# Retention's values by seven products of halves, and GpSimd as issuer of three kinds of transfers

## The chip, the cores and the metric

One core of a Trainium2 chip runs the whole program in one launch. The metric is the device time of one execution in microseconds, as the median of several runs.

## The reference

Two blocks over 512 tokens of width 1024, all in float32. The first is one hybrid layer (gated MLP mixing, sparse attention, a linear recurrence, then a feed-forward network of width 2816). The second is two hybrid layers, and the change lies in those. Each of them does, cut to what matters:

```python
proj = h @ w_in
qa, ka, va, za, qr, kr, vr, zr, ga, gr = jnp.split(proj, SPLIT_POINTS, axis=-1)
# attention: three groups (window, dilation) of four heads, values va (512 x 1536)
y_att = o_att.reshape(B, S, ATT_OUT) * jax.nn.silu(za)
# retention: four heads, values vr (512 x 1024), 256 per head
o_ret = retention(qr, kr, vr, positions, ret_gn_w)
y_ret = o_ret * jax.nn.silu(zr)
merged = jax.nn.sigmoid(ga) * (y_att @ w_proj_attn) + jax.nn.sigmoid(gr) * (y_ret @ w_proj_ret)
return x + gate[:, None, :] * (merged @ w_out)
```

The change concerns `vr = h @ w_vr`: 512 tokens by 1024 inputs by 1024 outputs, once per layer.

## The kernel before, in words

**Precision.** Every large product is made of three matmuls: each operand is held as a rounded high half and a low half (`split`, L140: ScalarE writes the high half, L144; VectorE subtracts it from the source for the low one, L145), and high x high, high x low and low x high are added in PSUM. `load_w` (L188) brings one weight tile of 128 x 1024 (512 KB) by SP into a raw buffer `wr` and splits it into `wh` and `wl`, of which there are four. It runs at a higher priority, so weights are loaded and split some way ahead. Where a stage lends a pool (`self.rawp`), two of three raw tiles come from there, four more buffers.

**Two shapes of a product.** `F_` (L204) makes one tile of 128 outputs by 512 tokens: 8 slices of k x 3 matmuls, 24 for one weight tile. `T_` (L231) makes 512 tokens by 512 outputs in four PSUM banks: 8 slices x 4 token tiles x 3 = 96 matmuls on four weight tiles.

**Seven products of halves.** `TS_` (L311) makes 512 tokens by 1024 outputs from operands cut in halves of the tokens, of the inputs and of the outputs, by Winograd's form of Strassen's scheme: seven products of 256 tokens x 512 inputs x 512 outputs, each 2 weight tiles x 2 token tiles x 2 slices x 3 = 24 matmuls. Three of them work on the operand and the weights as they are, four on sums. The order is written out by hand at its end:

```python
product("a", A(0, 0), B(0, 0), True, lambda t, ps: nc.scalar.activation(e[t], ps, AF.Copy))
product("d", A(1, 1), Tx(3), True)
product("a", A(1, 0), B(0, 1), False, lambda t, ps: done(t, 0, ps))
product("b", Sx(1), Tx(1), True, lambda t, ps: add(u[t], e[t], ps))
product("c", Sx(0), Tx(0), True, p5)
product("b", Sx(2), Tx(2), False, p7)
product("a", Sx(3), B(1, 1), True, p3)
```

VectorE adds the products together (L343 to L359), six additions per token tile. Before, only the strided values of attention (`strided_v`, L1066, the second and third group of `va`) are made so. The sums of the operand (`H`, four sums in two halves each) are made there by GpSimd and VectorE (L1078 to L1086) and split. The sums of the weights are made beforehand: `weight_sums` (L364) loads four quarter tiles `q` by SP, does four subtractions on GpSimd (L375 to L378) and writes the results to DRAM by SP (L381), in four groups per pair of weights, with pauses between the steps that the caller gives (12, 16 and 12 in the feed-forward stage).

**Order of the work.** Side work is written as generators (`spawn`, `tick`); each yields the pause until its next step, on a clock that counts matmuls, and is stepped between matmuls of the main line. The instructions of each engine, and the transfers of each queue, are issued in one order that is fixed when the program is built. A later tile that takes the room of an earlier one waits for its last reader.

**Stages that matter here.** The first block's feed-forward (`ffn`, L826) runs 44 `F_` passes; beside it run `ada` (L649: 96 tiles of 256 KB through VectorE) and the weight sums of layer 0. In the second block (`block2`, L912) each layer does: `attention_v` (L1055), `strided_v`, `attention` (L1104), the first half of retention's values (`retention_v`, L1264, one `T_`), the projection of attention (L943 to L947), `retention` (L1275) and the gates with the projection of retention (L957 to L969). `retention` makes queries and keys of one head at a time (`qk`), gates (`zr`) and spawns a task per head (`core`); the second half of the values, another `T_`, stands in the middle:

```python
qk(0), qk(1), zr(0), qk(2), zr(1)
Vs[1] = self.retention_v(l, h, rv, 1)
qk(3), zr(2), zr(3)
```

The weight sums for layer 1 are made beside layer 0's gates. `rotary_tables` (L1021, cosine and sine for retention) is written at the end of attention in layer 0. In `strided_v`, SP writes the results to attention's value tiles by 32 transfers of 64 KB per layer (L1099).

## Time and profile before

| | |
|---|---|
| median of 3 runs | 2506.12 us (2503.55 to 2507.12) |
| profiled execution | 2504.22 us |
| its span, first to last instruction | 2502.2 us |
| granted clock of TensorE, mean | 0.999 |
| TensorE busy | 2479.7 us, 11784 matmuls |
| VectorE busy | 1457.6 us |
| ScalarE busy | 1072.2 us |
| GpSimd busy | 176.6 us |
| read from HBM, written | 273.86 MB, 21.00 MB |

A row of a timeline has the start (us from the first instruction), the length, the engine (PE is TensorE, PEld its weight load, DVE VectorE, ACT ScalarE, POOL GpSimd, SPq the queue of SyncE), the line of the kernel, the operation and the tiles, written as out<-in, with the number of instructions that were merged; in brackets the idle time before it and what ended that. Matmuls are named with the moving operand first, so `ps<-h,wh` is `F_` and `ps<-wh,h` is `T_` or one of the seven products. Their lengths overlap in the pipeline.

### The profile page before, as it was taken

What the parts mean: (1) busy time and instruction counts of PE and PEld (TensorE: products, weight loads), DVE (VectorE), ACT (ScalarE), POOL (GpSimd) and SP (SyncE); (2) the same over time, 40 slices, a digit from 0 to 9 for tenths busy, and PEclk for the clock granted to TensorE, in tenths of its full rate; (3) what the DMA queues carried; (4) which work ended last, traced back from release to release, by engine and by line L of the source; (5) the groups of instructions that cost most, each with busy time, mean ns of one, the idle gap of its engine ahead of it and who ended that gap; (6) DMA issues with size and microseconds to landing.
All of it is one profiled execution on the core that took longest, in us unless ns stands there. A gap on an engine that the chain in (4) does not pass through costs nothing.

```text
span 2502.2 us, 31293 instructions
## 1 busy us (share of the span) xinstructions
PE 2479.7 (99%) x11784; PEld 2044.0 (82%) x11784; DVE 1457.6 (58%) x2701; ACT 1072.2 (43%) x1834; POOL 176.6 (7%) x152
## 2 busy tenths in 40 slices
PE   9999999999999999999999999999999999999998
PEld 7877777888888888888888788888888888888887
DVE  6567665776656788326633536764484343375635
ACT  4477766875334323224444532333253344223323
POOL 0023332000000110001100000003020000000000
PEclk9999999999999999999999999999999999999999
DMA  5522222223345797334432222226444222222233
GB/s 180 171 84 79 68 74 93 94 91 105 118 133 173 264 309 257 127 131 152 161 112 84 65 91 78 91 80 223 143 171 154 89 84 67 94 76 93 68 101 118
DMA packets 110216, 309.54 MB, mean 124 GB/s; under 512 B 14553, under 2 KB 20569, under 8 KB 109938
## 3 DMA queue, kind: packets, MB, share of 16 engines
q1 hardware_dynamic: 109344, 306.31, 37.8%
q8 instruction: 92, 1.51, 0.2%
q10 hardware_dynamic: 722, 1.25, 0.1%
q14 instruction: 58, 0.48, 0.1%
HBM read 273.86 MB, written 21.00 MB: 118 GB/s over the span
## 4 chain that ended last, share of the span: by engine, by line
PE 89%; DVE 4%; ACT 3%; DMA 2%; issue 1%; POOL 0%; ACTq 0%; DVEq 0%; POOLq 0%
PE ps L129 86%; PE ps L138 3%; DVE wl L145 1%; DMA wr<-in_w_out_dram 1%; ACT S L1539 1%; ACT wh L144 1%; DMA wr<-in_w_o_dram 0%; DVE H L145 0%; DVE yr L145 0%; POOL S L1546 0%; ACT S L1544 0%; DVE PTl L145 0%; DVE S L1533 0%; DMA wr<-in_w_mg_dram 0%; POOL X L1084 0%
## 5 line engine op out<-in xcount | busy, mean ns | idle before, releaser
L129 PE MATMUL ps<-h,wh 128*128 128x512 f32 (+1 forms) x4000 | 1243.4, 390 | 0.0
L129 PEld LDWEIGHTS ps<-h,wh 128*128 128x128 f32 x4000 | 734.2, 188 | 139.8 <-issue 5.1
L145 DVE TENSOR_TENSOR wl<-wr,wh 128x1024 fp32r<-128x1024 f32 x395 | 491.2, 1246 | 491.4 <-ACT wh L144 490.6
L129 PE MATMUL ps<-h,wl 128*128 128x512 f32 (+1 forms) x2000 | 772.9, 386 | 0.0
L144 ACT ACTIVATE wh<-wr 128x1024 fp32r<-128x1024 f32 x395 | 417.4, 1059 | 793.5 <-PE ps L129 563.4
L129 PEld LDWEIGHTS ps<-h,wl 128*128 128x128 f32 x2000 | 375.9, 188 | 75.3 <-DVE wl L145 0.4
L129 PE MATMUL ps<-wh,h 128*128 128x512 f32 x672 | 212.5, 393 | 0.2 <-ACT h L144 0.2
L129 PEld LDWEIGHTS ps<-wh,h 128*128 128x128 f32 x672 | 126.9, 189 | 27.5 <-DVE h L145 0.8
L129 PE MATMUL ps<-wl,h 128*128 128x512 f32 x336 | 131.8, 392 | 0.9 <-DVE wl L145 0.9
L129 PE MATMUL ps<-y,wh 128*128 128x512 f32 x384 | 119.2, 391 | 0.0
L665 DVE SCALAR_TENSOR_TENSOR acc<-aw,cact,acc 128x512 f32<-128x512 f32 x96 | 77.7, 810 | 21.2 <-DMA aw<-in_w_ada_dram 19.2
L129 PE MATMUL ps<-wh,f 128*128 128x512 f32 x288 | 89.6, 389 | 0.0
L1546 POOL TENSOR_SCALAR S<-S,sm 128x128 f32<-128x128 f32 (+3 forms) x64 | 69.6, 1099 | 212.4 <-ACT Q L144 87.4
L129 PEld LDWEIGHTS ps<-y,wh 128*128 128x128 f32 x384 | 71.5, 188 | 14.3
L375 POOL TENSOR_TENSOR q<-q,q 128x512 f32<-128x512 f32 x8 | 12.4, 1550 | 983.1 <-PE ps L138 487.6
L129 PE MATMUL ps<-yr,wh 128*128 128x512 f32 x256 | 78.8, 389 | 0.0
L145 DVE TENSOR_TENSOR PTl<-ps,PTh 128x512 fp32r<-128x512 f32 (+1 forms) x96 | 65.1, 684 | 22.5 <-ACT PTh L144 21.6
L1539 ACT ACTIVATE S<-S,sm 128x128 f32<-128x128 f32 (+3 forms) x128 | 70.2, 550 | 18.5 <-DVE sm L1537 18.4
L144 ACT ACTIVATE PTh<-ps 128x512 fp32r<-128x512 f32 (+1 forms) x96 | 56.1, 588 | 48.9 <-PE ps L138 43.9
L1138 DVE CUSTOM_DVE_ANT_0 P<-ps,c_masks 128x128 f32<-128x128 f32 (+1 forms) x96 | 31.1, 324 | 76.5 <-PE ps L129 59.5
L129 PEld LDWEIGHTS ps<-wl,h 128*128 128x128 f32 x336 | 63.6, 189 | 14.7 <-DVE wl L145 1.7
L129 PE MATMUL ps<-y,wl 128*128 128x512 f32 x192 | 74.7, 389 | 0.0
(363 smaller groups left out, 3293.6 us busy)
## 6 DMA issues: line engine op xcount, KB each, us to landing
aw<-in_w_ada_dram SPq DMA_DIRECT2D x96, 256.0 KB, 4.8
wr<-in_w_qk_dram SPq DMA_DIRECT2D x48, 512.0 KB, 3.5
wr<-in_w_ffn_in_dram SPq DMA_DIRECT2D x44, 512.0 KB, 4.5
wr<-in_w_g_dram SPq DMA_DIRECT2D x32, 512.0 KB, 3.5
wr<-in_w_qr_dram SPq DMA_DIRECT2D x32, 512.0 KB, 3.5
wr<-in_w_mg_dram SPq DMA_DIRECT2D x24, 512.0 KB, 3.8
wr<-in_w_ffn_out_dram SPq DMA_DIRECT2D x22, 512.0 KB, 3.4
wr<-in_w_va_dram SPq DMA_DIRECT2D x20, 512.0 KB, 4.6
```

The source lines that it names most:

```text
L129: self.nc.tensor.matmul(out, a, b, start=start, stop=stop, skip_group_check=True)
L138: self.nc.tensor.transpose(out, in_, self.ident[:k, :k])
L144: nc.scalar.activation(hi, src, AF.Copy)
L145: nc.vector.tensor_sub(lo, src, hi.bitcast(F32))
L375: g.tensor_sub(b11, b12, b11)
L665: v.scalar_tensor_tensor(acc, w, self.cact[:, k:k + 1], acc, op0=ALU.mult, op1=ALU.add)
L1138: v.tensor_tensor_reduce(dst, pv, mask, 1.0, -3e38, ALU.add, ALU.max, mx[:, n:n + 1])
L1539: nc.scalar.activation(Ps[h], Ps[h], AF.Exp, scale=0.125, bias=nm_[:, h:h + 1], accum_out=ls[:, h:h + 1])
L1546: nc.gpsimd.tensor_scalar(Ps[h], Ps[h], r[:, h:h + 1], None, op0=ALU.mult)
```

## The change

It makes retention's values of a layer by `TS_` in one stage, where two `T_` calls stood.

- `retention_v` now makes both halves. It reuses the four operand sums that `strided_v` made: there GpSimd stores each `H` to DRAM (`keep`, eight transfers of 512 KB per layer, spread over the stage), and here SP reads them back into six buffers. The first half of the values is kept in the four tiles that it had before; the second half is split and written to DRAM by SP (`vdr`), and read back in `retention` where the second `T_` stood.
- The sums of the weights of `vr` are made as well: for layer 0 beside the feed-forward stage, behind those of `va` (eight groups, pauses 7, 9, 6 in place of four with 12, 16, 12); for layer 1 beside layer 0's retention, in half width (`w=256`, eight groups). Those of `va` for layer 1 stay where they were.
- The transfers of `weight_sums` (loads and stores), of `keep`, and of the strided values into attention's tiles are issued by GpSimd (`g.dma_start`), where SP issued them.
- `rotary_tables` moves from the end of attention to the end of `retention_v`, in a pool `vs` that lies where attention's values lay and also lends four raw weight buffers.

```diff
--- before.py
+++ after.py
@@ -361,15 +361,15 @@
         product("b", Sx(2), Tx(2), False, p7)
         product("a", Sx(3), B(1, 1), True, p3)
 
-    def weight_sums(self, src, dst, pool, pace):
+    def weight_sums(self, src, dst, pool, pace, w=512):
 
         g = self.nc.gpsimd
         for i in range(2):
-            for o in (slice(0, 512), slice(512, D)):
+            for o in (slice(a, a + w) for a in range(0, D, w)):
                 q = []
                 for half, c in ((0, i), (1, i), (1, 2 + i), (0, 2 + i)):
-                    q.append(pool.tile([P, 512], F32, tag=f"q{len(q)}", name=self.nm("q"), bufs=1))
-                    self.nc.sync.dma_start(out=q[-1], in_=src[half][c][:, o])
+                    q.append(pool.tile([P, w], F32, tag=f"q{len(q)}", name=self.nm("q"), bufs=1))
+                    g.dma_start(out=q[-1], in_=src[half][c][:, o])
                 yield pace[0]
                 b11, b12, b22, b21 = q
                 g.tensor_sub(b11, b12, b11)
@@ -378,14 +378,16 @@
                 g.tensor_sub(b21, b21, b22)
                 yield pace[1]
                 for j, t in enumerate((b11, b22, b12, b21)):
-                    self.nc.sync.dma_start(out=dst[2 * j + i][:, o], in_=t)
+                    g.dma_start(out=dst[2 * j + i][:, o], in_=t)
                 yield pace[2]
 
-    def all_weight_sums(self, l, pool, pace):
+    def value_sums(self, l, names, pool, pace, w=512):
+
         A = self.A
-        for n, src in (("va", [A["w2_va"][l, g] for g in (1, 2)]),):
+        src = dict(va=[A["w2_va"][l, g] for g in (1, 2)], vr=[A["w2_vr"][l, g] for g in range(2)])
+        for n in names:
             self.w_sums[n, l] = self.dp.tile([8, P, D], F32, tag=f"{n}{l}", name=f"{n}{l}")
-            yield from self.weight_sums(src, self.w_sums[n, l], pool, pace)
+            yield from self.weight_sums(src[n], self.w_sums[n, l], pool, pace, w)
 
     def room(self, x):
 
@@ -837,7 +839,7 @@
                 self.ada_init(pool[0])
                 self.spawn(self.ada(pool[0], 1.9))
                 self.w_sums = {}
-                self.spawn(self.all_weight_sums(0, pool[0], (12.0, 16.0, 12.0)))
+                self.spawn(self.value_sums(0, ("va", "vr"), pool[0], (7.0, 9.0, 6.0)))
             if i % 2 == 0:
                 t = pool[0].tile([P, S], F32, tag="ft", name=self.nm("ft"), bufs=3)
                 nc.scalar.activation(t, ps, AF.Tanh, scale=0.5)
@@ -935,11 +937,12 @@
             mrg = [mp.tile([P, S], F32, tag="m", name=self.nm("m"), bufs=8) for _ in range(8)]
             with tc.tile_pool(name="att", bufs=1, side="right", reuse_waits="tile") as ap:
                 self.attention(l, h, ap, vp, V, ya, mrg)
-                if l == 0:
-                    self.rotary_tables(ap, "qk", 4)
             e_v.close()
             with tc.tile_pool(name="retv", bufs=1, side="right", reuse_waits="tile") as rv:
-                W = self.retention_v(l, h, rv, 0)
+                with tc.tile_pool(name="vrs", bufs=1, reuse_waits="tile") as vs:
+                    self.rawp = vs
+                    W = self.retention_v(l, h, rv, vs)
+                    self.rawp = None
                 for c in range(4):
                     w = self.load_w(A["w2_pa"][l, c])
                     for i in (2 * c, 2 * c + 1):
@@ -948,14 +951,17 @@
                 e_ya.close()
                 yo, e_yo = op("yro")
                 yr = self.new_op(yo, "yr")
-                with tc.tile_pool(name="ret", bufs=1, reuse_waits="tile") as rp:
+                with tc.tile_pool(name="ret", bufs=1, reuse_waits="tile") as rp, \
+                        tc.tile_pool(name="rq", bufs=1, side="right", reuse_waits="tile") as rq:
+                    if l == 0:
+                        self.spawn(self.value_sums(1, ("vr",), rq, (4.0, 5.0, 4.0), 256), 20.0)
                     self.retention(l, h, rp, rv, W, yr)
             mo, e_mo = op("mop")
             m = self.new_op(mo, "mo")
             with tc.tile_pool(name="rt2", bufs=1, side="right", reuse_waits="tile") as rp:
                 T = {}
                 if l == 0:
-                    self.spawn(self.all_weight_sums(1, rp, (6.0, 9.0, 5.0)))
+                    self.spawn(self.value_sums(1, ("va",), rp, (6.0, 9.0, 5.0)))
                 for i in range(11):
                     c = i - 3
                     if i < 8:
@@ -1069,6 +1075,7 @@
         for g in (1, 2):
             for c in range(4):
                 V[g, c] = vp.tile([P, 512], F32, tag="V", name=self.nm("V"), bufs=12)
+        self.h_sums = self.dp.tile([4, 2, P, D], F32, tag="hsums", name=self.nm("hsums"))
         x_ = lambda: sp.tile([P, S], F32, tag="X", name=self.nm("X"), bufs=8)
         R, H = {}, {}
         for p in range(2):
@@ -1090,16 +1097,26 @@
                 o = slice(p * 512, p * 512 + 512)
                 self.split(H[j][0][:, o], H[j][1][:, o], R[p][j])
 
+        def keep():
+            yield 12.0
+            for j in (1, 0, 2, 3):
+                for x, y in zip(H[j], self.h_sums[j]):
+                    g_.dma_start(out=y, in_=x.bitcast(F32))
+                    yield 2.0
+
+        kept = self.spawn(keep())
+
         def done(t, half, z):
             x = z
             if t < 2 and half == 0:
                 x = x_()
                 nc.scalar.activation(x, z, AF.Copy)
             for c in range(4):
-                nc.sync.dma_start(out=V[1 + half, c][t * 32:t * 32 + 32, :], in_=x[c:P:4, :])
+                g_.dma_start(out=V[1 + half, c][t * 32:t * 32 + 32, :], in_=x[c:P:4, :])
 
         self.TS_(h, [self.A["w2_va"][l, g] for g in (1, 2)], self.w_sums["va", l],
                  lambda j, k, t, lo: H[j][lo][:, k * 256 + t * P:k * 256 + t * P + P], x_, done)
+        self.wait(kept)
 
     def attention(self, l, h, ap, vp, V, ya, mrg):
 
@@ -1261,15 +1278,30 @@
         self.wait()
 
 
-    def retention_v(self, l, h, rv, half):
-        V = []
-
-        def done(t, ps):
-            vt = rv.tile([P, 2, 512], F32R, tag="V", name=self.nm("V"), bufs=4)
-            self.split(vt[:, 0, :], vt[:, 1, :], ps)
-            V.append(vt)
-
-        self.T_(self.tok(h), self.A["w2_vr"][l, half], 8, done, outer=2)
+    def retention_v(self, l, h, rv, vs):
+
+        nc = self.nc
+        self.vdr = self.dp.tile([4, P, D], F32, tag="vdr", name=self.nm("vdr"))
+        V = [rv.tile([P, 2, 512], F32R, tag="V", name=self.nm("V"), bufs=4) for _ in range(4)]
+        H = {}
+        for j in (1, 0, 2, 3):
+            H[j] = [vs.tile([P, D], F32R, tag="H", name=self.nm("H"), bufs=6) for _ in range(2)]
+            for x, y in zip(H[j], self.h_sums[j]):
+                nc.sync.dma_start(out=x.bitcast(F32), in_=y)
+
+        def done(t, half, z):
+            if half == 0:
+                self.split(V[t][:, 0, :], V[t][:, 1, :], z)
+                return
+            y = vs.tile([P, 2, 512], F32R, tag="Y", name=self.nm("Y"), bufs=2)
+            self.split(y[:, 0, :], y[:, 1, :], z)
+            nc.sync.dma_start(out=self.vdr[t], in_=y.rearrange("p a b -> p (a b)").bitcast(F32))
+
+        self.TS_(h, [self.A["w2_vr"][l, i] for i in range(2)], self.w_sums["vr", l],
+                 lambda j, k, t, lo: H[j][lo][:, k * 256 + t * P:k * 256 + t * P + P],
+                 lambda: vs.tile([P, S], F32, tag="X", name=self.nm("X"), bufs=6), done)
+        if l == 0:
+            self.rotary_tables(vs, "X", 6)
         return V
 
     def retention(self, l, h, rp, rv, V, yr):
@@ -1356,7 +1388,9 @@
 
         box = {}
         qk(0), qk(1), zr(0), qk(2), zr(1)
-        Vs[1] = self.retention_v(l, h, rv, 1)
+        Vs[1] = [rv.tile([P, 2, 512], F32R, tag="V", name=self.nm("V"), bufs=4) for _ in range(4)]
+        for t, x in enumerate(Vs[1]):
+            nc.sync.dma_start(out=x.rearrange("p a b -> p (a b)").bitcast(F32), in_=self.vdr[t])
         qk(3), zr(2), zr(3)
         self.wait()
```

## Rows read from the trace of the kernel before

**Rows 1.** The page: span, busy time by engine, chain that ended last.

```profile
span 2502.2 us, 31293 instructions
...
PE 2479.7 (99%) x11784; PEld 2044.0 (82%) x11784; DVE 1457.6 (58%) x2701; ACT 1072.2 (43%) x1834; POOL 176.6 (7%) x152
...
PE 89%; DVE 4%; ACT 3%; DMA 2%; issue 1%; POOL 0%; ACTq 0%; DVEq 0%; POOLq 0%
```

**Rows 2.** Timeline of TensorE, layer 0, retention's first half and the work after it.

```profile
1472.99 0.39 PE L129 MATMUL ps<-wh,h 128*128 128x512 f32 x1
...
1494.75 0.62 PE L129 MATMUL ps<-ya,wh 128*128 128x512 f32 x2
```

**Rows 3.** Strided stage: busy us (PE, PEld, DVE, ACT, POOL), clock, DMA share, GB/s.

```profile
1197.00:1237.00 40.00, 39.58 (x175) 32.41 (x174) 34.66 (x38) 20.83 (x27) 4.11 (x3) 1.00 0.54 169
```

**Rows 4.** Waits of TensorE in the whole kernel: us, times, longest.

```profile
PE ps L129 <- DVE wl L145: 3.0, 5, 0.9
```

**Rows 5.** VectorE by line, whole kernel: busy us, mean ns, idle before.

```profile
L145 DVE TENSOR_TENSOR wl<-wr,wh 128x1024 fp32r<-128x1024 f32 x395 | 491.2, 1246 | 491.4 <-ACT wh L144 490.6
...
L145 DVE TENSOR_TENSOR V<-ps,V 128x512 fp32r<-128x512 f32 x20 | 13.8, 688 | 21.2 <-ACT V L144 21.2
...
L346 DVE TENSOR_TENSOR X<-X,ps 128x512 f32<-128x512 f32 x4 | 2.6, 680 | 0.0
```

**Rows 6.** Issues of transfers: count, KB each, median us to landing.

```profile
q<-in_w_va_dram SPq DMA_DIRECT2D x32, 256.0 KB, 4.8
va<-q SPq DMA_DIRECT2D x32, 256.0 KB, 4.2
...
wr<-in_w_vr_dram SPq DMA_DIRECT2D x16, 512.0 KB, 3.4
...
V<-X SPq DMA_DIRECT2D x64, 64.0 KB, 2.1
```

**Rows 7.** Timeline of TensorE, layer 0, attention's last products with the values.

```profile
1450.20 1.14 PE L129 MATMUL ps<-PT,V 128*128 128x128 f32 x8
```

**Rows 8.** Timelines of GpSimd and SP's queue, layer 0's strided stage.

```profile
1203.02 1.68 POOL L1086 TENSOR_TENSOR X<-X,X 128x512 f32<-128x512 f32 x1 [1.76 <-DVE X L1085]
...
1231.98 15.12 SPq L1099 DMA_DIRECT2D V<-X  x24
```

**Rows 9.** Timeline of GpSimd, feed-forward stage: first subtractions of three groups.

```profile
822.98 1.30 POOL L375 TENSOR_TENSOR q<-q,q 128x512 f32<-128x512 f32 x1 [386.73 <-DVE cact L644]
...
895.09 2.14 POOL L375 TENSOR_TENSOR q<-q,q 128x512 f32<-128x512 f32 x1 [25.42 <-DMA q<-in_w_va_dram]
...
932.43 1.29 POOL L375 TENSOR_TENSOR q<-q,q 128x512 f32<-128x512 f32 x1 [30.76 <-DMA q<-in_w_va_dram]
```

**Rows 10.** Timelines of VectorE and TensorE, feed-forward stage: two splits, its end.

```profile
958.87 1.22 DVE L145 TENSOR_TENSOR wl<-wr,wh 128x1024 fp32r<-128x1024 f32 x1
...
1024.96 1.23 DVE L145 TENSOR_TENSOR wl<-wr,wh 128x1024 fp32r<-128x1024 f32 x1 [3.61 <-ACT wh L144]
...
1051.04 0.63 PE L129 MATMUL ps<-acc,onesr 128*4 128x512 f32 x2
```

**Rows 11.** Columns as in rows 3: the feed-forward stage.

```profile
840.00:860.00 20.00, 20.00 (x90) 16.58 (x89) 18.44 (x24) 6.22 (x8) 0.00 (x0) 1.00 0.95 328
...
980.00:1051.00 71.00, 71.00 (x314) 58.47 (x314) 35.97 (x44) 23.00 (x30) 0.00 (x0) 1.00 0.39 126
840.00:980.00 140.00, 140.00 (x619) 115.72 (x618) 118.15 (x150) 40.94 (x52) 17.33 (x12) 1.00 0.90 303
```

**Rows 12.** Splits of weights from 960.2 to 1026.3: durations, first, last start.

```profile
L145 DVE TENSOR_TENSOR wl<-wr,wh x14: 1214/1224/1226, 963.5 to 1025.0; 128x1024 fp32r<-128x1024 f32 x14
```

**Rows 13.** Reads of attention's value tiles: durations, first and last start.

```profile
L129 PEld LDWEIGHTS ps<-PT,V x192: 186/192/192, 1402.6 to 2110.9; 128*128 128x128 f32 x192
```

**Rows 14.** Columns as in rows 3: two stretches of layer 0's retention.

```profile
1585.00:1595.00 10.00, 10.00 (x48) 8.26 (x47) 8.66 (x22) 3.13 (x4) 0.00 (x0) 1.00 0.16 52
1625.00:1635.00 10.00, 10.00 (x46) 8.29 (x45) 2.84 (x3) 2.63 (x3) 0.00 (x0) 1.00 0.20 68
```

## The prediction, made before the changed kernel ran

> **What bounds the kernel now.** I read the page first, then TensorE's own timeline where retention's values are made, then the stages that have to pay for the change. The page says that TensorE is busy 99% of the span and makes up 89% of the chain that ended last [rows 1]: a microsecond goes when TensorE has less to do, or comes when it must wait. How fast it goes is read from the timeline: in layer 0 the first half of retention's values starts at 1472.99 and the next work at 1494.75 [rows 2]. That is 21.76 us for 96 matmuls (8 slices of k, 4 tiles of tokens, 3 terms), 226.7 ns each with no gap. The 390 ns that the page gives for one matmul is its length in the pipeline, not its price.
>
> The same seven products already run in the strided values of attention, so their stage is the nearest row for the new one: in 40.00 us TensorE ran 175 matmuls and idled 0.42 us, with VectorE busy 34.66 us and the transfers at 169 GB/s [rows 3]. All waits of TensorE for the low half of a weight come to 3.0 us in the whole kernel, 0.9 us the longest [rows 4].
>
> **What goes.** Two halves of 96 matmuls a layer become seven products of 24: 192 to 168. 24 x 226.7 ns = 5.44 us a layer, **10.88 us** for both. This count is certain.
>
> **What comes beside TensorE in the new stage** (168 x 226.7 ns = 38.1 us). Every product splits two weights, so 14 where the two halves together split 8. VectorE: 14 x 1.246 = 17.4 us, eight splits of results of 0.688 (5.5 us) and twelve additions of 0.680 (8.2 us) [rows 5], 31.1 us of 38.1, 82%. The strided stage, with its operand sums on top, had 87% and lost 0.42 us [rows 3]. ScalarE gets six more splits and two copies a layer; it was busy 20.83 us of 40 in that same row. I charge between nothing and 0.5 us a layer, and take 0.3, as the new stage comes out of one-weight passes of 5.44 us, with its buffers full: **0.6 us** for both.
>
> Transfers: 14 weights, eight operand sums read back and four value tiles written, each of 512 KB like a weight [rows 6], 13.6 MB. Six of the eight operand tiles fit at once; they lie where attention's values lay, whose last reader runs at 1450.20 [rows 7], 22 us before the stage. Their first use is in the fourth product, 16.3 us into it. The other two wait for the product that reads sum 1 (21.8 us in) and are needed at 32.6 us. What queues behind them on SP are weights, four of which are split ahead. Cost 0; the upper bound is below, as a rival. The second half's value tiles come back by four reads on SP, after heads 0 and 1 have let go of the buffers; the 96 matmuls that stood there go, and heads 2 and 3 follow queries and keys as before. The rotary tables, some 17 VectorE operations of at most 0.69 us, move from attention's end behind the products; the 21.8 us of the attention projection lie between them and their first reader: 0.
>
> **What GpSimd and the feed-forward stage must carry.** Before, GpSimd issued no transfer, so no row has its price. The ends: SP's strided writes went out in 15.12 us for 24, 0.63 us each [rows 8]; a GpSimd instruction on one 128x512 tile took from 1.29 to 2.14 us [rows 9]. I take 1.29, since it is GpSimd's own row. A group of weight sums (four loads, four subtractions, four stores) is then 8 x 1.29 + 5.5 of arithmetic + 4.8 and 4.2 of landing [rows 6] = 24.8 us; with 0.63 it is 19.5, with 2.14 31.6. Eight groups stand in the feed-forward stage where four stood. Counted from 822.98 [rows 9], the last begins its arithmetic at 822.98 + 7 x 24.8 = 996.6 and has landed some 15 us later; with 2.14 at 1063. TensorE ends the stage's passes at 1051.04 [rows 10], and the last weight is split 19.4 us ahead of its pass (ended 1026.19, pass from 1051.04 - 5.44): even the late end is covered. 0.
>
> These groups bring 8.39 MB more, while the transfers already run at 303 GB/s and 0.90 busy from 840 to 980, 328 at their best; from 980 to 1051 they fall to 126 [rows 11]. The extra takes 8.39 MB / 328 to / 303 GB/s = 25.6 to 27.7 us of transfer time. In this stage the weights do fall behind: the one that was split by 960.09 [rows 10] has 14 splits after it [rows 12], so its pass begins at 1051.04 - 15 x 5.44 = 969.4. Its lead is 9.3 us, where the last one has 19.4. Between no delay (the calm stretch alone could take (303 - 126) x 71 us = 12.6 MB) and all 27.7 us on the weights, I take a third, since a weight of 0.52 MB in 5.44 us is 96 of the 303 GB/s: 9.2 us, just inside the lead. 0. SP also sheds 64 issues and its waits for GpSimd's results; that frees a queue that does not bound anything, so I credit nothing. GpSimd's added subtractions can hold a VectorE operation by their own length, 16 x 1.29 = 21 us at most; VectorE has 118 of 140 us taken there [rows 11], so the lead covers this too.
>
> In the strided stage GpSimd is free from 1204.70 [rows 8] and issues 8 stores of operand sums and 32 of values, 52 us at 1.29, 86 at 2.14. It ends near 1260 or 1295; attention reads these values first at 1402.6 [rows 13]. 0. In layer 0's retention eight groups of half width (about 22 us each) keep GpSimd busy for some 177 us. VectorE there runs between 8.66 and 2.84 us of 10 [rows 14], and the stretch of 2.84 is the one that disappears; heads' tasks are written with several us between their steps, and no wait of TensorE stands there. 0, with up to 1 us as the other end.
>
> **The sum.** The profiled execution took 2504.22 us (span 2502.2, 2.0 around it), 1.9 below the median of the runs. 2504.22 - 10.88 + 0.6 = 2493.9; from the median, 2506.12 - 10.3 = **2495.8**, 0.41% less.
>
> **Rivals.** (a) *The new stage is starved of transfers.* All 13.6 MB fall into it, at the best rate seen, 328 GB/s: 41.6 us for 38.1, 3.5 us a layer. For it: twice the strided stage's rate. Against: the operands can start 22 us early. 2495.8 + 7.0 = 2502.8, the same within what can be told. (b) *The feed-forward stage stalls.* All the extra transfer time falls on the weights, because a second queue takes its share ahead of SP's: 27.7 - 9.3 = 18.4 us of TensorE, **2514.2**, slower. It decides from 9.3 us of delay on. For it: the lead did shrink by 10 us already; against: the weights are a third of the traffic. (c) *GpSimd's transfers crawl.* If a group keeps the step of before, (932.43 - 822.98) / 3 = 36.5 us [rows 9], the eighth begins its arithmetic at 1078.5 and has landed by about 1093, 42 us after the stage. The next stage's rows, loaded by SP into the same room, hold the weights behind them: 42 - 19.4 = 22.6 us, 2518. For it, only that VectorE works 84% of this stage; against it, that the old step followed from pauses of 40 between groups, now 22. The Trainium skill, SBUF — State Buffer, Summary: rules for kernel authors, speaks for (c): a transfer issued from GpSimd has its descriptors made there and starves while VectorE holds the shared port in its two-port modes, so such transfers belong on SP or ScalarE. The Trainium skill counts there, in Who interferes with whom, copies, casts and tensor-scalar operations among those that take these modes, and an operation on two tensors not; no run shown here has a transfer issued from GpSimd to try it on. By that rule the sum would be (c)'s.
>
> **How the numbers follow.** Chances: forecast 0.70, (a) 0.13, (b) 0.11, (c) 0.06. About 0.2% is what a measurement of this kernel can tell from no change, 5 us. The forecast is faster; (a) is the same; of (b) a third, where only part of the delay gets through, is the same, the rest with (c) slower: 0.70, 0.17, 0.13. The low end lets the strided stages lose their 0.42 us too and a run lie 2.6 under the median as the fastest did: 2506.1 - 10.9 - 0.8 - 2.6 = 2491.8. The high end takes in (a) and a partial (b): 2505.
>
> **What would show it.** Right: 11736 matmuls; retention's products without a gap in about 38 us a layer; feed-forward passes still 5.44 us apart; attention's start as before. Wrong: TensorE waiting for a weight's low half in the feed-forward stage (b) or in retention's products (a); GpSimd's last feed-forward group after the stage's end (c). A loss anywhere else would be one that I did not see.

## The result: slower by 0.78%, and the profile after

The changed kernel takes 2524.76 us (median of 5 runs, 2524.35 to 2525.83), the kernel before 2505.96 in the same session: ratio 1.0078, 95% interval 1.0066 to 1.009. The forecast was 2495.8, its range ended at 2505. First the page of the changed kernel, lines that answer to [rows 1], and two of its queue section and one of its list of issues.

```profile
span 2523.1 us, 31594 instructions
...
PE 2479.9 (98%) x11736; PEld 2039.5 (81%) x11736; DVE 1514.5 (60%) x2737; ACT 1085.4 (43%) x1848; POOL 352.4 (14%) x440
...
q0 software_dynamic: 15104, 46.15, 5.3%
...
PE 80%; DVE 8%; DMA 6%; ACT 3%; issue 2%; POOL 1%; ACTq 0%; DVEq 0%; POOLq 0%
...
V<-X POOLq DMA_DIRECT2D x64, 64.0 KB, 4.5
```

The 48 matmuls are gone (11784 to 11736), yet the span is 20.9 us longer, and TensorE's share of the chain fell from 89% to 80%. GpSimd (POOL) is busy twice as long and now has a queue with 46.15 MB. TensorE's waits (us in all, times, longest) name two places, where [rows 4] had one line of 3.0 us:

```profile
PE ps L129 <- DVE wl L145: 19.0, 13, 5.0
PE ps L129 <- ACT qk L1170: 6.1, 2, 3.2
```

Where the time went is read from the first matmul of each stage in TensorE's timeline. The table has the length of each stage in us; "mix" is an experiment told below.

| from, to | before | after | sums on SP (e1) | mix (e5) |
|---|---|---|---|---|
| start to end of feed-forward's 44 passes | 1051.5 | 1072.1 | 1051.9 | 1052.1 |
| to layer 0's first product with an operand sum | 162.1 | 162.1 | 162.1 | 162.1 |
| layer 0, to the projection of attention | 281.2 | 300.4 | 299.8 | 295.6 |
| layer 0, to the projection of retention | 229.9 | 209.7 | 222.5 | 211.1 |
| to layer 1's first product with an operand sum | 152.1 | 154.2 | 154.9 | 153.2 |
| layer 1, to the projection of attention | 277.8 | 299.0 | 298.2 | 294.5 |
| layer 1, to the projection of retention | 230.0 | 208.2 | 208.2 | 208.2 |
| rest | 117.6 | 117.4 | 116.7 | 116.6 |

Retention's new products are as forecast: 168 x 226.7 ns in place of 96 adds 16.3 us to a stage "to the projection of attention", and the 96 that went take 21.8 out of the next. Against that, after lost 20.6 us in the feed-forward stage, 2.9 and 4.9 more at attention's two starts, 2.1 on the way to layer 1 and 1.6 in layer 0's retention: 32.1 - 10.9 - 0.2 (in the rest) = 21.0. Layer 0's 2.9 is a net figure. Before, TensorE waited twice in layer 0's attention, at 1402.60 and 1423.32, for copies on ScalarE; ahead of the copy that ended the first wait ScalarE's timeline has a table load of 1.28 us, next to the sine and cosine of the rotary tables. Layer 1, which makes no tables, has neither wait. With the tables moved both are gone, 2.5 us, in the changed kernel and in its variants below. Line of TensorE's waits, kernel before:

```profile
PE ps L129 <- ACT PT L1203: 2.5, 2, 1.3
```

**The feed-forward stage.** Windows of the changed kernel (columns as in [rows 3]); the last one is retention's new stage.

```profile
840.00:860.00 20.00, 20.00 (x90) 16.57 (x89) 18.69 (x18) 6.78 (x9) 14.21 (x19) 1.00 0.90 323
...
880.00:900.00 20.00, 18.34 (x81) 14.82 (x80) 17.97 (x19) 4.43 (x6) 12.16 (x16) 1.00 1.00 359
900.00:920.00 20.00, 12.69 (x54) 9.53 (x52) 17.86 (x18) 5.41 (x7) 13.32 (x15) 0.99 0.99 353
...
920.00:925.00 5.00, 3.90 (x9) 2.75 (x10) 4.90 (x5) 0.00 (x0) 4.27 (x6) 0.50 0.86 277
...
1517.00:1557.00 40.00, 40.00 (x178) 33.11 (x177) 35.60 (x51) 16.19 (x19) 6.84 (x10) 1.00 0.64 211
```

The transfers are full (share 1.00, 359 GB/s; the most before was 0.95 and 328, [rows 11]) and GpSimd is busy, its issues counted, 12 to 14 of each 20 us, where it had 17 of 140 [rows 11]. TensorE idles for 14.0 us in five stalls between 885 and 943, each for a weight's low half. After the longest its granted clock stood at 0.50 of full, the 1.2 GHz level, from 920 to 925; with 0.96 from 915, 0.86 to 930 and 0.66 from 940 to 945 that is another 5.1 us ((1 - clock) x 5 us, added). Together that is at most 19.1 of the 20.6, since the clock was already low in the last 1.5 us of the longest stall.

How one stall comes about, from the timelines of SP's queue, VectorE, ScalarE and TensorE:

```profile
906.08 3.48 SPq L666 DMA_DIRECT2D aw<-in_w_ada_dram  x5
910.36 0.33 SPq L193 DMA_DIRECT2D wr<-in_w_ffn_in_dram  x1
911.62 7.57 SPq L666 DMA_DIRECT2D aw<-in_w_ada_dram  x5
921.08 0.33 SPq L193 DMA_DIRECT2D wr<-in_w_ffn_in_dram  x1
...
917.19 1.65 DVE L667 SCALAR_TENSOR_TENSOR acc<-aw,cact,acc 128x512 f32<-128x512 f32 x1
918.76 2.28 DVE L145 TENSOR_TENSOR wl<-wr,wh 128x1024 fp32r<-128x1024 f32 x1
...
918.31 1.06 ACT L144 ACTIVATE wh<-wr 128x1024 fp32r<-128x1024 f32 x1 [0.38 <-DMA wr<-in_w_ffn_in_dram]
...
921.10 0.80 PE L129 MATMUL ps<-h,wl 128*128 128x512 f32 x1 [4.98 <-DVE wl L145]
```

SP issues the weight at 910.36, behind five loads for `ada`, and ScalarE's split of it can't start before 918.31, 8 us later (4.8 is the median landing of these weights). Then its low half takes VectorE 2.28 us in place of 1.22. The next weight leaves 10.7 us after this one, since five `ada` loads wait for VectorE to free their buffers; a pass takes 5.44.

VectorE's two groups from 820 to 960, by shape (busy us, mean ns), in the kernel before and then in the changed one:

```profile
L665 DVE SCALAR_TENSOR_TENSOR acc<-aw,cact,acc 128x512 f32<-128x512 f32 x73 | 60.5, 829 | 20.7 <-DMA aw<-in_w_ada_dram 19.2
L145 DVE TENSOR_TENSOR wl<-wr,wh 128x1024 fp32r<-128x1024 f32 x25 | 31.5, 1259 | 3.4 <-ACT wh L144 3.3
```

```profile
L667 DVE SCALAR_TENSOR_TENSOR acc<-aw,cact,acc 128x512 f32<-128x512 f32 x67 | 64.9, 970 | 10.3 <-DMA aw<-in_w_ada_dram 9.0
L145 DVE TENSOR_TENSOR wl<-wr,wh 128x1024 fp32r<-128x1024 f32 x20 | 30.9, 1545 | 5.2 <-ACT wh L144 5.2
```

SP's waits for `ada`'s buffers in that stretch (us, times, longest), before and then after:

```profile
SPq L664 <- DVE acc L665: 22.8, 37, 1.5
```

```profile
SPq L666 <- DVE acc L667: 58.0, 65, 5.4
```

And GpSimd's timeline there, which answers to [rows 9]: first subtraction of groups 1, 2, 5 and 8, and one store.

```profile
820.45 1.27 POOL L375 TENSOR_TENSOR q<-q,q 128x512 f32<-128x512 f32 x1 [2.83 <-DMA q<-in_w_va_dram]
822.02 0.57 POOL L381 DMA_DIRECT2D va<-q  x1 [0.30 <-POOL q L375]
...
834.81 1.77 POOL L375 TENSOR_TENSOR q<-q,q 128x512 f32<-128x512 f32 x1 [2.74 <-DMA q<-in_w_va_dram]
...
881.47 1.28 POOL L375 TENSOR_TENSOR q<-q,q 128x512 f32<-128x512 f32 x1 [1.08 <-DMA q<-in_w_vr_dram]
...
932.43 1.67 POOL L375 TENSOR_TENSOR q<-q,q 128x512 f32<-128x512 f32 x1 [2.28 <-DMA q<-in_w_vr_dram]
```

A group starts every (932.43 - 820.45) / 7 = 16.0 us. The pauses written in the code fix only where an instruction stands in its own engine's order; with nothing else to issue here, GpSimd goes as fast as its buffers come free.

**The attention's start.** Timeline of ScalarE, changed kernel: the copies of queries and keys come behind four splits that wait for their weights.

```profile
1270.87 1.06 ACT L144 ACTIVATE wh<-wr 128x1024 fp32r<-128x1024 f32 x1 [2.59 <-DMA wr<-in_w_qk_dram]
1273.55 1.06 ACT L144 ACTIVATE wh<-wr 128x1024 fp32r<-128x1024 f32 x1 [1.61 <-DMA wr<-in_w_qk_dram]
1274.51 1.07 ACT L1170 ACTIVATE qk<-ps 128x512 f32<-128x512 f32 x2
```

### The profile page after: what moved, and what is told of

Read it like the earlier page. It is cut to its first block, busy times and chain, and to the rows that moved or that the text cites. A ratio compares the mean times of both kernels' runs of the same rounds, so it can differ in the third digit from the quotient of the medians.

```text
span 2523.1 us, 31594 instructions
## 1 busy us (share of the span) xinstructions
PE 2479.9 (98%) x11736; PEld 2039.5 (81%) x11736; DVE 1514.5 (60%) x2737; ACT 1085.4 (43%) x1848; POOL 352.4 (14%) x440
## 3 DMA queue, kind: packets, MB, share of 16 engines
q0 software_dynamic: 15104, 46.15, 5.3%
## 4 chain that ended last, share of the span: by engine, by line
PE 80%; DVE 8%; DMA 6%; ACT 3%; issue 2%; POOL 1%; ACTq 0%; DVEq 0%; POOLq 0%
PE ps L129 78%; PE ps L138 3%; DVE wl L145 2%; DMA aw<-in_w_ada_dram 1%; DVE acc L667 1%; DMA wr<-in_w_va_dram 1%; DMA wr<-in_w_out_dram 1%; ACT wh L144 1%; DMA wr<-in_w_qk_dram 1%; ACT S L1573 1%; DMA wr<-in_w_ffn_in_dram 1%; DMA wr<-in_w_o_dram 0%; DVE H L145 0%; DMA V<-X 0%; POOL V L1115 0%
## 5 line engine op out<-in xcount | busy, mean ns | idle before, releaser
L145 DVE TENSOR_TENSOR wl<-wr,wh 128x1024 fp32r<-128x1024 f32 x407 | 512.5, 1264 | 475.3 <-ACT wh L144 474.4
L144 ACT ACTIVATE wh<-wr 128x1024 fp32r<-128x1024 f32 x407 | 429.4, 1059 | 793.5 <-PE ps L129 509.4
L129 PE MATMUL ps<-wh,h 128*128 128x512 f32 x512 | 161.6, 393 | 0.2 <-ACT h L144 0.2
L129 PEld LDWEIGHTS ps<-wh,h 128*128 128x128 f32 x512 | 96.5, 189 | 21.1 <-DVE h L145 0.8
L129 PE MATMUL ps<-wl,h 128*128 128x512 f32 x256 | 100.4, 392 | 0.9 <-DVE wl L145 0.9
L667 DVE SCALAR_TENSOR_TENSOR acc<-aw,cact,acc 128x512 f32<-128x512 f32 x96 | 86.7, 904 | 11.6 <-DMA aw<-in_w_ada_dram 9.7
L372 POOL DMA_DIRECT2D q<-in_w_va_dram x32 | 17.4, 545 | 457.7 <-DVE h L145 378.1
L129 PE MATMUL ps<-wh,H 128*128 128x512 f32 x256 | 79.4, 389 | 0.0
L372 POOL DMA_DIRECT2D q<-in_w_vr_dram x48 | 25.7, 539 | 302.1 <-DVE ra L1046 277.1
```

The costliest lines, as they stand in the source:

```text
L129: self.nc.tensor.matmul(out, a, b, start=start, stop=stop, skip_group_check=True)
L144: nc.scalar.activation(hi, src, AF.Copy)
L145: nc.vector.tensor_sub(lo, src, hi.bitcast(F32))
L372: g.dma_start(out=q[-1], in_=src[half][c][:, o])
L667: v.scalar_tensor_tensor(acc, w, self.cact[:, k:k + 1], acc, op0=ALU.mult, op1=ALU.add)
```

## The experiments

"After" is the changed kernel. Ratios are to the kernel before, measured beside each.

**e1, weight sums' transfers on SP.** Edit of after:

```diff
-                    g.dma_start(out=q[-1], in_=src[half][c][:, o])
+                    self.nc.sync.dma_start(out=q[-1], in_=src[half][c][:, o])
-                    g.dma_start(out=dst[2 * j + i][:, o], in_=t)
+                    self.nc.sync.dma_start(out=dst[2 * j + i][:, o], in_=t)
```

> The changed kernel with the transfers of the weight sums issued by SP again; all else as changed. Theory O (own queue): issued by GpSimd, the sums' transfers are no longer held to their place among SP's loads, while SP's vacant places are taken by loads of w_ada, which now stand ahead of the feed-forward weights (54 before the 21st weight, 38 in the kernel before). Then SP issuing them brings the weights back: the stage's passes end near 1051 to 1057 us (1071.9 in the changed kernel), the median near 2503 to 2507. Rival B (bytes): the 8.4 MB of the added sums are what the stage can't carry, whoever issues them: end at 1065 or later, median 2518 or more. Rival D (VectorE): GpSimd's 32 subtractions hold VectorE up: they are all still there, end at 1060 or later, median 2512 or more.

2516.33 us, ratio 1.0047 [1.0032, 1.0062]. The whole loss of the feed-forward stage is gone (1051.9) with the same bytes and the same subtractions in it, so the 8.39 MB by themselves are not its cause, nor are the 32 subtractions by themselves: rivals B and D fall. The median misses theory O's range all the same, since layer 0's retention grew by 12.8 us over after (table), with a new stall of 8.8 us at 1601.5. e11 takes that up.

**e2, before with only its weight sums issued by GpSimd.** The same two lines the other way round, in the kernel before.

> The kernel before with one part of the change alone: GpSimd issues the transfers of its weight sums (four groups, no added bytes). SP's order is then that of the changed kernel, with 54 loads of w_ada ahead of the 21st feed-forward weight. Theory O: the weights' lead shrinks to nothing and TensorE stalls in the feed-forward stage, 3 to 15 us: median 2509 to 2521. Rival B: no byte is added, so no stall: 2504 to 2508. Rival D: the same 16 subtractions, only denser: under 3 us, 2505 to 2509.

2505.85 us, ratio 1.0003 [0.9994, 1.0012]: no change. The weights' lead (end of a low half's split to the first matmul that reads it, from the two timelines) fell from 15 to 19 us to 2.8 to 3.8 for weights 14 to 22, and no stall came of it: theory O had the lead right and the stalls wrong. Four groups issued by GpSimd eat the reserve; it takes more to break it.

**e3, after without its 32 subtractions in the feed-forward stage.** Transfers and SP's order stay; layer 0's weight sums are left out of the computation.

```diff
-                g.tensor_sub(b11, b12, b11)
+                if not skip:
+                    g.tensor_sub(b11, b12, b11)
```

(and so for the other three).

> The changed kernel without GpSimd's 32 subtractions of the feed-forward stage; its transfers stay, and SP's order with them. The sums that it writes are the plain quarter tiles. Rival D (VectorE held by the subtractions): the stall goes, end of the passes by 1055, time 2502 to 2507. Theories O and B: TensorE still waits for the low halves of weights, 8 us or more, end at 1062 or later, 2514 to 2525.

2510.45 us in one run, between the ranges of the theories. The stage ends at 1059.1: 13.0 of the 20.6 us go with the subtractions. VectorE's two groups from 820 to 960 here, and then the window:

```profile
L671 DVE SCALAR_TENSOR_TENSOR acc<-aw,cact,acc 128x512 f32<-128x512 f32 x80 | 60.0, 750 | 20.3 <-DMA aw<-in_w_ada_dram 19.2
L145 DVE TENSOR_TENSOR wl<-wr,wh 128x1024 fp32r<-128x1024 f32 x22 | 26.7, 1215 | 5.5 <-ACT wh L144 5.5
```

```profile
820.00:960.00 140.00, 136.78 (x675) 115.57 (x674) 106.77 (x143) 41.24 (x54) 32.38 (x60) 0.99 0.95 350
```

Without GpSimd's arithmetic the mean `acc` is 750 ns (970 in after) and the mean `wl` 1215 (1545). 7.6 us stay. Some 2.1 of them came before the stage (its first pass starts at 825.57, in the kernel before at 823.46), the other 5.4 in the two passes with the stalls of 1.33 and 1.89 and a lowered clock; in after the passes lose 19.7. The transfers ran at 350 GB/s, more than after's 318 in the same stretch, so their rate alone doesn't make the large stalls.

**e4, strided values issued by SP.** Edit of after: `g_.dma_start(out=V[...` becomes `nc.sync.dma_start(out=V[...`.

> The changed kernel with the strided values written by SP again; GpSimd keeps the sums' and the operand sums' transfers. Theory Q: with GpSimd as issuer the order on ScalarE puts more weight splits ahead of attention's first copies of queries and keys, and TensorE waits for these 3.2 and 2.9 us in the two layers; by SP both waits go: median 2518 to 2520. Rival: attention's start is late because the operand sums' stores and the weights crowd the transfers there; then the waits stay, 2523 to 2526.

2514.87 us (2510.73 to 2520.24), ratio 1.004 [1.0027, 1.0052], 9.9 under after, more than theory Q had. Attention's stalls of 3.16 and 2.93 shrink to at most 0.9; layer 0's stage is 296.5 us in place of 300.4, layer 1's 295.8 in place of 299.0. Of the 11.0 us between the two profiled spans these make 7.1; another 2.3 lie in the feed-forward stage and 2.1 on the way to layer 1, which the edit doesn't touch. With e9, which is 5.5 under e8 by the same edit, the move is worth 5 to 10 us. ScalarE here:

```profile
1259.35 0.60 ACT L1170 ACTIVATE qk<-ps 128x512 f32<-128x512 f32 x1 [2.03 <-PE ps L129]
1266.45 0.60 ACT L1170 ACTIVATE qk<-ps 128x512 f32<-128x512 f32 x1 [6.50 <-DMA V<-X]
```

The second copy waits for a strided write: its tile takes the room of an `X` that is still being written out. So these writes are wanted at attention's start, by whoever takes their room, long before attention reads the values. In after they also land later (4.5 us in the list of issues above, 2.1 in [rows 6]), and ScalarE's order has its splits ahead of the copies. Which of the two weighs more was not tried apart.

**e5, the mix.** After, with SP as issuer of layer 0's sums (an argument `e=nc.sync` in `weight_sums`) and of the strided values; GpSimd keeps layer 1's sums and the operand sums.

> The changed kernel with two of its moves undone: SyncE issues layer 0's weight sums in the feed-forward stage again (GpSimd keeps layer 1's, in the retention and the stage after it), and SyncE issues the strided values. Theory P (each move to GpSimd did harm only where it let other work pass ahead: the sums in the feed-forward stage, the strided values at the attention's start; the retention's sums are better on GpSimd): the feed-forward stage ends near 1052 as before, the strided stage and attention take 296.5 a layer, the retention 209 a layer without the 8.8 us stall of the run with all sums on SyncE, so 2494 to 2499 in all. Rival B (the 8.39 MB added still cost somewhere when the issuers are put back): 2502 to 2506. Rival S (the stall in the retention came from the new arrangement of the feed-forward stage and not from SyncE issuing the sums there): 2504 to 2509, with a stall near 1600.

**2495.42 us** (2494.85 to 2496.98), ratio **0.9962** [0.995, 0.9975]: as the theory had it, and faster than both kernels. Its page:

```profile
span 2493.4 us, 31593 instructions
...
PE 2470.4 (99%) x11736; PEld 2034.7 (82%) x11736; DVE 1502.8 (60%) x2737; ACT 1085.5 (44%) x1848; POOL 290.0 (12%) x312
```

**e6, everything issued by SP.** Edits of e1 and e4 together, and `nc.sync` in `keep()`, which writes the operand sums.

> The changed kernel with every moved transfer (weight sums, operand sums, strided values) issued by SyncE. Theory P: the feed-forward stage ends near 1052, the attention starts with stalls under 1.5 us, but layer 0's retention keeps a stall of 6 to 9 us and some loss of clock because SyncE waits there for GpSimd's subtractions ahead of weight loads: 2506 to 2512. Rival S (that stall is not SyncE's wait): under 2500. Rival G (GpSimd's issues are worth time by themselves, spread over many waits): over 2514.

2524.27 us, ratio 1.0076 [1.0061, 1.0092]: slower by 12 us than theory P allowed, as slow as after. The retention stall is there (9.31 us), but attention's starts got new stalls of 6.88 and 6.25, where P had under 1.5. P had not counted the operand sums, which e10 takes by themselves.

**e7, three buffers for `ada`'s weights in place of five.** One number in after.

> The changed kernel with 3 buffers in place of 5 for the ada weights, so that SyncE's order has 42 of their loads ahead of the 21st feed-forward weight in place of 54 (before the change: 38 of them and 20 sum transfers); GpSimd's transfers and subtractions are untouched. Theory V (the stalls come of GpSimd's subtractions holding VectorE, closely packed since its own queue runs free; the order only took the reserve): the feed-forward stage ends at 1062 to 1072, 2515 to 2525 in all. Rival R (the stalls come of ada loads ahead of the weights): it ends at 1051 to 1056, and the time is 2503 to 2509.

2530.81 us, ratio 1.0104 [1.009, 1.0118], the stage ends at 1078.3: R falls, and V's range was passed too, so neither theory had this run right. SP's waits from 820 to 960, and then its timeline:

```profile
SPq L666 <- DVE acc L667: 52.0, 56, 2.8
...
SPq L666 <- DMA aw<-in_w_ada_dram: 26.4, 13, 5.3
```

```profile
893.36 10.51 SPq L666 DMA_DIRECT2D aw<-in_w_ada_dram  x4
905.79 0.33 SPq L193 DMA_DIRECT2D wr<-in_w_ffn_in_dram  x1
```

With 42 `ada` loads ahead of the 21st weight in place of 54, four of them hold SP for 10.5 us, and the weight behind them leaves at 905.79. So it isn't how many stand ahead alone; how long SP stands in them counts.

**e8, GpSimd held to its place.** After, with GpSimd still the issuer; four one-column copies per group read the newest feed-forward operand:

```diff
+                    if hold and self.held:
+                        g.tensor_copy(q[-1][:, 0:1], self.held[-1][:, 0, 0:1].bitcast(F32))
                     g.dma_start(out=q[-1], in_=src[half][c][:, o])
```

> The changed kernel, GpSimd still issuing every sum's transfer, but with a one-column copy on GpSimd ahead of each load of layer 0's sums that reads the latest feed-forward operand, so that a group can't start before its place in the stage. SyncE's built order is the same as in the changed kernel (54 ada loads ahead of the 21st weight). Theory V (the loss comes of GpSimd running through the eight groups by 945 us, with dense subtractions and transfers beside the ada work): the groups spread past 980, the stage ends at 1052 to 1058, 2503 to 2509 in all. Rival R (the order of SyncE's loads): the stage still ends past 1065 and the time stays above 2515. Rival C (the added bytes whatever their pace): stalls as before, moved later, over 2515.

2506.53 us, ratio 1.0009 [1.0, 1.0018]; the stage ends at 1057.1. GpSimd's timeline (the copy, with its wait ahead of group 2; groups 2 and 8) and the one stall left in TensorE's:

```profile
858.28 1.83 POOL L373 COPY q<-f 128x1 f32<-128x1 f32 x4 [31.06 <-ACT f L147]
...
867.65 1.68 POOL L377 TENSOR_TENSOR q<-q,q 128x512 f32<-128x512 f32 x1 [5.47 <-DMA q<-in_w_va_dram]
...
1023.79 1.29 POOL L377 TENSOR_TENSOR q<-q,q 128x512 f32<-128x512 f32 x1 [2.19 <-DMA q<-in_w_vr_dram]
...
967.96 0.79 PE L129 MATMUL ps<-h,wl 128*128 128x512 f32 x1 [3.36 <-DVE wl L145]
```

As V had it; R and C fall. Same issuer, same bytes, same subtractions, same order on SP: spread over 204 us in place of 112 (first subtraction of group 1 to that of group 8), they cost 5.6 us in place of 20.6. Pace is the cause of 15.0. SP's waits for VectorE in the stretch from 820 to 960 are as long as in after (58.0 us), yet TensorE has no stall there:

```profile
SPq L668 <- DVE acc L669: 57.7, 82, 3.2
```

So these waits don't make the stalls by themselves; they take the lead. It falls to 5 us at weight 19 and to 0.1 at the 29th, the one that stalls (measured as in e2), and in e1 it stays at 12 us and more from the 12th weight on, with no stall. From 950 to 970 the chain of work through that stall spends 55% of its time in two `ada` loads. That the remaining 5.6 us are the price of SP's order fits this, but was not tried apart: GpSimd's fifth group runs there too.

**e9, e8 and e4 together.**

> As e8_held, and SyncE issues the strided values again. Theory V: the two gains add, about 9 us below e8_held and 2495 to 2500, level with the mix whose feed-forward sums SyncE issues. Rival R: over 2506.

2501.07 us, ratio 0.9987 [0.9977, 0.9996], 5.5 under e8 and just above the range. The two gains add for the most part; the mix stays ahead.

**e10, the mix with the operand sums issued by SP.** `g_` to `nc.sync` in `keep()`.

> The mix (e5), with the operand sums' eight transfers a layer issued by SyncE in place of GpSimd. Theory P (these belong on GpSimd: on SyncE they wait for VectorE's H tiles ahead of the next weights and the strided values): a stall of 6 to 7 us near each attention's start, 6 to 16 us over the mix, 2502 to 2511. Rival (the stalls of the run with everything on SyncE came of the sums or of their sum): within 2 us of the mix.

2511.05 us, ratio 1.0023 [1.0013, 1.0032], 15.6 over the mix; stalls of 6.64 and 5.97 at the two starts. SP's queue and ScalarE's timeline:

```profile
1224.09 7.76 SPq L193 DMA_DIRECT2D wr<-in_w_qk_dram  x2
1232.83 15.78 SPq L1116 DMA_DIRECT2D V<-X  x24
1248.70 6.65 SPq L193 DMA_DIRECT2D wr<-in_w_qk_dram  x3
...
1252.68 1.06 ACT L144 ACTIVATE wh<-wr 128x1024 fp32r<-128x1024 f32 x1 [4.89 <-DMA wr<-in_w_qk_dram]
```

In the mix SP issues four of attention's weights ahead of the 24 strided writes. With eight operand sums ahead of them there are two, and TensorE waits for the third. SP waited for the operand sums' own tiles only 2.8 us (from 1190 to 1262), so what counts is their place in the order more than the waits that theory P named. These transfers are worth having on GpSimd.

**e11, the mix with the retention's sums issued by SP.** `nc.sync` as issuer of layer 1's `vr` sums.

> The mix (e5), with layer 1's retention sums issued by SyncE, in layer 0's retention. Theory P (SyncE waits there for GpSimd's subtractions ahead of weight loads): a stall of 6 to 9 us near 1600 and 10 to 14 us over the mix, 2505 to 2510. Rival S (the stall of e1 and e6 came of what went before): within 2 us of the mix.

2508.54 us, ratio 1.0014 [1.0004, 1.0023], 13.1 over the mix. SP's waits in layer 0's retention and TensorE's in the whole kernel, and then ScalarE's timeline:

```profile
SPq L382 <- POOL q L376: 17.4, 8, 3.5
SPq L382 <- POOL q L378: 11.6, 8, 2.5
...
PE ps L129 <- ACT rh L144: 10.6, 3, 9.4
```

```profile
1596.23 1.06 ACT L144 ACTIVATE wh<-wr 128x1024 fp32r<-128x1024 f32 x1 [13.95 <-DMA wr<-in_w_qr_dram]
```

SP stands at the stores until GpSimd has subtracted, with weight loads behind them; ScalarE stands 13.95 us for the weight, whose split comes at 1596.23 (in the mix at 1584.43), and the next head's rotated operand waits behind its split on ScalarE. So S falls. The same stall is e1's 8.8 and e6's 9.31. The two prices also account for e6: 2495.4 + 15.6 + 13.1 = 2524.1, measured 2524.27.

## Why the prediction was wrong

**Right:** the 10.88 us of removed matmuls (e5 shows 8.8 of them in the span, 2493.4 against 2502.2); retention's new stage without a gap (40.00 of 40 us busy above, so rival (a) fell, and the 0.6 us charged was not needed); and, nearly, layer 0's retention on GpSimd (0 to 1 us forecast; 1.6 in after, 3.0 in the mix). That the mix lands on the forecast's number, 2495.42 against 2495.8, is in part luck: the 2.5 us of the rotary tables, which were not forecast, pay for most of those 3.0.

**Wrong, the step that failed:** the feed-forward stage at 0. The prediction weighed three things there singly against one lead of 9.3 us: the transfers ("a third ... 9.2 us, just inside the lead. 0"), GpSimd's subtractions ("the lead covers this too") and SP's order ("a queue that does not bound anything, so I credit nothing"). They come together and in one stretch, and the lead is not a fixed store: e2, which adds no byte and no subtraction, takes it from 15 to 19 us down to about 3 by the issuer alone. Three sizes under it were off.
- *The group step.* 24.8 us was taken, from 1.29 us an issue, the row of an arithmetic instruction. The issues took 0.54 and 0.57 us, below the low end of 0.63, and a group 16.0 us. It was the shorter step that hurt: it packs 32 subtractions and 16.8 MB into some 130 us. The worry had been a late end, 1063.
- *The subtractions.* They don't hold VectorE for 16 x 1.29 us once, but lengthen much of what it does beside them: `wl` 1259 to 1545 ns, `acc` 829 to 970 in that stretch. e3 prices that at 13.0 us, in one run. The Trainium skill, SBUF — State Buffer, Who interferes with whom, says that a VectorE instruction with both inputs in SBUF contends with a GpSimd instruction that reads SBUF, and that the order of issue decides which of the two is blocked; the prediction cited from there only that such an operation doesn't take the two-port modes. e3 agrees with the fuller rule: 1215 ns without the subtractions.
- *SP's order.* The places of the 64 issues that left were not empty time: `ada` loads moved up into them (54 ahead of the 21st weight in place of 38), and SP waits there for VectorE, 58.0 us in place of 22.8. That empties the lead (e2, e8), and the stalls come when packed groups meet an empty one. e1, which puts the transfers back on SP, keeps the lead and loses nothing in this stage.

**Rival (b)** had the place and nearly the size (18.4 us, 20.6 measured) and the wrong mechanism: the bytes on a second queue. e8 has both and loses 5.6.

**Rival (c)** was wrong on its facts: GpSimd's transfers did not crawl, all eight groups were done by 945 us. The Trainium skill's rule beside it (SBUF — State Buffer, Summary: rules for kernel authors), that transfers issued by GpSimd starve while VectorE is in its two-port modes, was not put to the test: the two largest groups of VectorE's work beside after's groups (`acc` and `wl` above) have two tensors as inputs, and the prediction itself says that the page doesn't count an operation on two tensors there. With VectorE working 18 of each 20 us, no starving showed. Its advice to issue from SP was right for two of the four moves here, on other grounds, and the other two speak against it (e10, e11).

**The second miss:** attention's start at 0, "attention reads these values first at 1402.6". The first to need these transfers is not the reader of the values, but the copies that take the room of their source tiles, some 150 us earlier; in after those copies also stand behind four splits on ScalarE. It cost 4.9 us at layer 1's start and 2.9 net at layer 0's; e4 and e9 put the price of the move at 5 to 10 us in all. A smaller miss went the other way: the rotary tables' move, put at 0, gave back the 2.5 us told above.

**Not settled:** how much of the 20.6 us is each of the lengthened VectorE work and the transfers' slower landing when both are there (e3 removes the first alone, but a packed stretch without its transfers was not tried); and what the 2.1 us on the way to layer 1 are, where the other runs show between 0 and 3.

## What to carry to other kernels

In these runs a queue was also a pacer: work moved from a shared queue to one of its own lost the waits that spread it, ran as fast as its buffers allowed, and what stood behind it on the old queue moved up. Ask of every moved transfer what it will be ahead of in the old queue, and what it will be beside in time. Here one kind of transfer was better moved (those that on the shared queue stood ahead of weight loads, or held them while waiting for another engine's result: 13 to 16 us each) and another better left (those that keep a side task at its stage's pace, or whose room is wanted soon: 20 us, and 5 to 10); with every one on GpSimd the kernel was 0.78% slower than before, with every one on SP 0.76%, with two on each 0.38% faster.

## What was not expected of the hardware

- GpSimd's issue of a 256 KB transfer took 0.54 to 0.57 us here, no more than SP's 0.63 for a strided 64 KB one [rows 8]. Landing was longer for the strided ones when GpSimd issued them: 4.5 us against 2.1.
- A 128x1024 subtraction on VectorE that takes 1.22 us took 2.28 beside GpSimd's subtractions (918.76 above).
- TensorE's granted clock read 0.50 from 920 to 925, around the end (921.10) of a stall of 4.98 us; the stall's price was more than its length.
